# A hybrid decoder trunk: the Strassen products of the FFN's second matrix in another order and with other signs, the sums of its blocks formed by accumulating DMA loads

## The chip, the cores and the metric

One core of one Trainium2 chip. The metric is device time in microseconds (us) of one execution of the whole program; lower is better. The kernel before takes 2162.08 us (median of 3 runs, 2161.11 to 2162.54).

## The reference

Two layers (an mLSTM mixer in the first, a Mamba-2 mixer in the second), each between two half-step SwiGLU FFNs, so four FFNs in all; batch 1, 512 tokens, model width 1024, FFN width 2816, all float32. The change touches the FFN alone:

```python
def swiglu(h, w1, w3, w2):
    return (jax.nn.silu(h @ w1) * (h @ w3)) @ w2

def sublayer(x, fn, g_pre, g_post, shift, scale, gate, weight):
    hmod = rms_norm(x, g_pre) * (1 + scale[:, None, :]) + shift[:, None, :]
    y = rms_norm(fn(hmod), g_post)
    return x + weight * gate[:, None, :] * y
```

## The kernel before

Every matmul is three float32r matmuls (`mm3`, L184 to L188): each operand is split into a high part (ScalarE's copy, L191 or L174) and a low part (VectorE's subtraction, L192 or L175), and high by high, low by high and high by low are added in PSUM. Weights come through a pool of 4 buffers (`rawp`, 128 x 1024 floats, 512 KB) by loads on the SP queue, are split into `wh` and `wl` (pools of 3) or into held slots, and the `raw` buffer is free once VectorE's subtraction has read it. The Tile scheduler orders each engine's instructions; the engines then run them in that order and wait on semaphores.

An FFN (class `Ffn`) has two stages.

**The up-projections** (`first`, `rest`, `tile_in`): 22 tiles of 128 of the FFN's width, each 48 matmuls for w1 and w3. A pair of tiles j (11 pairs) makes an operand of 512 tokens by 256 for w2. `factors(j)` forms the token-side factors of a Strassen scheme over two token halves by two tiles and splits them; three are used at once, four are kept.

**The products with w2.** w2's rows of a pair j fall into two tiles e, its columns into two halves c, so there are four blocks of 128 x 512 floats (256 KB), written here B[e,c]. DRAM holds them as `w2[l, h, c, j]`, a row of 1024 floats for both tiles e. Each of the seven Strassen products is 6 matmuls of 128 x 512 for each j (two token blocks by `mm3`). PSUM has eight banks: four `aux` and four `mm`.

- `flush` (L670 to L687), once for each j while the up-projections run: loads w2(0,j) and w2(1,j) (two loads of 512 KB), adds B00 to B01 (L679), adds B11 to B00 and to B10 (L681, one instruction over 1024), splits, and makes products 1, 7 and 6.
- `outp`, after the last tile (here called the tail): `five(j)` loads B11 (256 KB) for product 5; the loop with L732 loads w2(1,j), subtracts B11 from B01 and makes product 3; the loop with L753 and L759 loads w2(0,j), subtracts B00 from B10 and makes product 4, and for four of the j at once product 2 (of B00). For the other seven j (`HELD = 7`) B00's split is held in slots, and their product 2 comes last, for one token block after the other.
- Between them VectorE and ScalarE combine the PSUM banks into the output rows (L722 to L724, L738 to L740, L767 to L783). `Post.evac` and `Post.finish` square, sum, scale and add to x; `Pre.tok` then transposes the new x on TensorE (L346) for the next stage, whose first weights' matmuls run on the first half of the tokens (`HA`) before the second (`HB`).

So the tail's TensorE work is 4 products for 11 pairs and one last `flush` of 3: 47 x 6 = 282 matmuls. GpSimd (POOL) makes no DMA.

```python
        def halves(self, raw, n=2 * T):
            wh = whp.tile([P, 1024], F32R, tag="wh", name="wh")
            wl = wlp.tile([P, 1024], F32R, tag="wl", name="wl")
            split(wh[:, :n], wl[:, :n], raw[:, :n])
            return [(wh[:, k * T:k * T + T], wl[:, k * T:k * T + T]) for k in range(n // T)]
```

Of the kernel before, what the change touches and what calls it, by code (L numbers as in the profile page):

```python
# [9 lines left out]
F32 = mybir.dt.float32  # L10
# [5 lines left out]
P = 128  # L16
# [19 lines left out]
HELD = 7  # L36
# [20 lines left out]
def trunk(ctx: ExitStack, tc: tile.TileContext, i: dict, out: bass.AP):  # L57
# [475 lines left out]
    class Ffn:  # L533
# [91 lines left out]
        def factors(self, j):  # L625
# [5 lines left out]
            tt(raw[:, :T], s0, s1, ALU.add)  # L631
            tt(raw[:, T:T + H], s0[:, lo], s1[:, hi], ALU.add)
# [5 lines left out]
            for n, (m, src) in enumerate(((1, raw[:, T:T + H]), (6, s0[:, hi]), (7, s1[:, lo]))):  # L638
# [4 lines left out]
            for (ma, a), (mb, b) in (((5, raw[:, lo]), (3, s0[:, lo])), ((2, raw[:, hi]), (4, s1[:, hi]))):  # L643
# [14 lines left out]
        def w2(self, c, j):  # L658
            raw = rawp.tile([P, 1024], F32, tag="raw", name="raw")
            nc.sync.dma_start(raw, i["w2"][self.l, self.h, c, j])  # L660
            return raw

# [40 lines left out]

        def outp(self, nxt):
            n = NF // 2
            m5 = [ps_mm(0), ps_mm(1)]

            def five(j):
                raw = rawp.tile([P, 1024], F32, tag="raw", name="raw")
                nc.sync.dma_start(raw[:, :T], i["w2"][self.l, self.h, 1, j, :, T:])  # L710
                with tc.high_priority():
                    b5, = self.halves(raw, T)
                self.product(m5, self.kept[j][5], b5, j == 0, j == n - 1)
            for j in range(n - 2):
                five(j)
# [4 lines left out]
            lo, hi = slice(0, T), slice(T, D)  # L720
            for t in range(2):
                act(yg[2 + t][:, hi], m[1][t], AF.Copy)  # L722
                tt(yg[t][:, lo], yg[2 + t][:, hi], m[7][t], ALU.add)
                tt(yg[2 + t][:, hi], yg[2 + t][:, hi], m[6][t], ALU.add)  # L724
            done_ps(*m[1], *m[6])
            for j in range(n - 2, n):
                five(j)
            m3 = [ps_aux(), ps_aux()]
            for j in range(n):
                raw = self.w2(1, j)  # L730
                with tc.high_priority():
                    tt(raw[:, lo], raw[:, lo], raw[:, hi], ALU.subtract)  # L732
                    b3, = self.halves(raw, T)
                self.product(m3, self.kept[j][3], b3, j == 0, j == n - 1)
                free(*self.kept[j]["53"])
            for t in range(2):
                act(yg[t][:, hi], m5[t], AF.Copy)
                tt(yg[t][:, lo], yg[t][:, lo], m5[t], ALU.subtract)  # L738
                tt(yg[t][:, hi], yg[t][:, hi], m3[t], ALU.add)
                tt(yg[2 + t][:, hi], yg[2 + t][:, hi], m3[t], ALU.add)  # L740
                post.evac(t, 1, yg[t][:, hi])
            done_ps(*m3)

            m4, m2 = [ps_aux(), ps_aux()], [ps_mm(2), ps_mm(3)]
            held = {}
            joint = range(3, 3 + 2 * (n - HELD), 2)
            hs = [j for j in range(n) if j not in joint]
            for j in range(n):
                raw = self.w2(0, j)
                k = self.kept[j]  # L750
                if j in joint:
                    with tc.high_priority():
                        tt(raw[:, hi], raw[:, hi], raw[:, lo], ALU.subtract)  # L753
                        b2, b4 = self.halves(raw)
                    self.product(m4, k[4], b4, j == 0, j == n - 1)
                    self.product(m2, k[2], b2, j == joint[0], False)
                    free(*k["24"])
                    continue
                tt(raw[:, hi], raw[:, hi], raw[:, lo], ALU.subtract)  # L759
                b4 = slot(F32R, "bh"), slot(F32R, "bl")  # L760
                split(*b4, raw[:, hi])
                held[j] = slot(F32R, "bh"), slot(F32R, "bl")
                split(*held[j], raw[:, lo])
                self.product(m4, k[4], b4, j == 0, j == n - 1)
                free(*b4)
# [680 lines left out]
```

## Time and profile before

| what | value |
|---|---|
| time, median of 3 | 2162.08 us |
| time of the profiled execution | 2159.1 us |
| its span | 2157.1 us |
| TensorE (PE) busy | 2061.5 us, 96% |
| VectorE (DVE) busy | 1625.5 us, 75% |
| ScalarE (ACT) busy | 1004.8 us, 47% |
| GpSimd (POOL) busy | 12.5 us, 1% |
| mean DMA rate | 160 GB/s, 346.08 MB |

The profiled execution lies 3 us under the median of the runs. Busy time is a union of an engine's instructions; a matmul of 128 x 512 is recorded with 0.36 to 0.42 us because its end is modelled and it overlaps the next, so the pace is read from counts in a stretch. "Idle before" is an engine's idle time just before instructions of a group, with what ended it. PEclk is the granted clock of TensorE as a share of 2.4 GHz.

### The profile page before, as it was taken

How to read it: one execution, taken by the hardware profiler on the slowest of the kernel's cores; microseconds unless marked ns; L12 is line 12 of the kernel's file. 1: busy time of each engine (PE TensorE's matmuls, PEld its weight loads, DVE VectorE, ACT ScalarE, POOL GpSimd, SP SyncE). 2: the span in 40 equal slices, each digit the busy share in tenths (PEclk: the TensorE clock that was granted, in tenths of full speed). 3: DMA queues.
4: the chain of work that ended last, by engine and by line, in shares of the span. 5: the costliest groups of instructions: out<-in, count | busy, mean ns of one | idle time of the engine just before them, and what ended most of it. 6: DMA issues, size and time to landing. Idle time of an engine off the chain costs nothing.

```text
span 2157.1 us, 28206 instructions
## 1 busy us (share of the span) xinstructions
PE 2061.5 (96%) x10422; PEld 1709.9 (79%) x10422; DVE 1625.5 (75%) x2699; ACT 1004.8 (47%) x1769; POOL 12.5 (1%) x33
## 2 busy tenths in 40 slices
PE   7999998899999999998999999799999999999997
PEld 5888886797789787866987887698788789888875
DVE  8969967857886888769777755878998857555558
ACT  5434434745463333336433433556656655333334
POOL 0000000000000000000000000000000000000000
PEclk9999999999999999998999999999999999999999
DMA  7556756345334677654457534524334332343344
GB/s 275 187 165 234 234 166 234 113 133 163 125 97 148 224 240 228 200 188 154 157 182 251 167 118 161 191 87 136 113 104 128 114 115 79 109 136 121 119 165 157
DMA packets 108986, 346.08 MB, mean 160 GB/s; under 512 B 13545, under 2 KB 13545, under 8 KB 108849
## 3 DMA queue, kind: packets, MB, share of 16 engines
q1 hardware_dynamic: 108848, 344.29, 49.4%
q8 instruction: 81, 1.33, 0.3%
q14 instruction: 57, 0.46, 0.1%
HBM read 342.00 MB, written 2.24 MB: 160 GB/s over the span
## 4 chain that ended last, share of the span: by engine, by line
PE 67%; DVE 15%; DMA 11%; ACT 4%; issue 3%; DVEq 0%; ACTq 0%; SPq 0%
PE mm L186 19%; PE mm L188 19%; PE mm L187 19%; DMA raw<-in_w 8%; DMA raw<-in_ada_w 2%; DVE wl L192 2%; PE aux L186 2%; DVE wl L175 2%; PE aux L187 2%; PE aux L188 2%; DVE acc L208 2%; ACT wh L174 1%; ACT wh L191 1%; PE aux L1156 1%; DVE raw L681 1%
## 5 line engine op out<-in xcount | busy, mean ns | idle before, releaser
L186 PE MATMUL mm<-hm,wh 128*128 128x512 f32 (+1 forms) x2128 | 771.4, 366 | 4.8 <-ACT hm L360 2.6
L188 PE MATMUL mm<-hm,wl 128*128 128x512 f32 (+1 forms) x2128 | 770.4, 363 | 3.3 <-DVE wl L175 3.2
L187 PE MATMUL mm<-hm,wh 128*128 128x512 f32 (+1 forms) x2128 | 770.1, 363 | 0.0
L174 ACT ACTIVATE wh<-raw 128x1024 fp32r<-128x1024 f32 (+1 forms) x294 | 278.8, 957 | 409.1 <-PE mm L187 131.9
L188 PEld LDWEIGHTS mm<-hm,wl 128*128 128x128 f32 x2128 | 404.0, 190 | 67.9 <-DVE wl L175 6.7
L186 PEld LDWEIGHTS mm<-hm,wh 128*128 128x128 f32 x2128 | 403.1, 191 | 69.0 <-ACT hm L360 3.8
L187 PEld LDWEIGHTS mm<-hm,wh 128*128 128x128 f32 x2128 | 404.6, 190 | 60.7 <-issue 1.4
L175 DVE TENSOR_TENSOR wl<-raw,wh 128x1024 fp32r<-128x1024 f32 (+1 forms) x294 | 320.5, 1096 | 118.5 <-ACT wh L174 114.8
L191 ACT ACTIVATE wh<-raw 128x1024 fp32r<-128x1024 f32 (+1 forms) x192 | 145.3, 763 | 299.0 <-PE mm L187 127.8
L192 DVE TENSOR_TENSOR wl<-raw,wh 128x1024 fp32r<-128x1024 f32 (+1 forms) x192 | 162.9, 854 | 48.8 <-ACT wh L191 46.5
L208 DVE SCALAR_TENSOR_TENSOR acc<-raw,csil,acc 128x1024 f32<-128x1024 f32 x112 | 143.5, 1282 | 44.6 <-DMA raw<-in_ada_w 43.9
L598 DVE TENSOR_TENSOR s<-s,mm 128x512 f32<-128x512 f32 (+1 forms) x97 | 59.7, 617 | 129.9 <-PE mm L188 129.9
L679 DVE TENSOR_TENSOR raw<-raw 128x512 f32<-128x512 f32 x44 | 30.4, 691 | 71.7 <-DMA raw<-in_w 71.5
L186 PE MATMUL aux<-wh,th 128*128 128x512 f32 x176 | 70.0, 406 | 10.5 <-ACT wh L191 10.5
L187 PE MATMUL aux<-wl,th 128*128 128x512 f32 x176 | 69.6, 396 | 0.0
L188 PE MATMUL aux<-wh,tl 128*128 128x512 f32 x176 | 69.5, 395 | 0.0
L191 ACT ACTIVATE kh<-s 128x256 fp32r<-128x256 f32 x88 | 36.5, 416 | 57.8 <-DVE s L598 50.5
L597 ACT ACTIVATE s<-mm 128x512 f32<-128x512 f32 (+1 forms) x97 | 51.3, 531 | 23.2 <-PE mm L188 23.2
L186 PE MATMUL mm<-wh,kh 128*128 128x512 f32 x120 | 48.1, 409 | 13.5 <-ACT wh L191 13.5
L187 PE MATMUL aux<-wl,kh 128*128 128x512 f32 x120 | 50.2, 418 | 9.3 <-DVE wl L192 7.8
L681 DVE TENSOR_TENSOR raw<-raw 128x1024 f32<-128x1024 f32 x44 | 53.8, 1222 | 1.1
L1049 DVE SCALAR_TENSOR_TENSOR cv<-mm,c_mb_cw,cv 128x511 f32<-128x511 f32 (+2 forms) x72 | 53.3, 742 | 0.6
(317 smaller groups left out, 3130.3 us busy)
## 6 DMA issues: line engine op xcount, KB each, us to landing
raw<-in_w SPq DMA_DIRECT2D x346, 512.0 KB, 4.3
raw<-in_ada_w SPq DMA_DIRECT2D x128, 512.0 KB, 4.0
raw<-in_mb_wx SPq DMA_DIRECT2D x24, 512.0 KB, 3.6
raw<-in_w SPq DMA_DIRECT2D x44, 256.0 KB, 2.8
a<-in_ada SPq DMA_DIRECT2D x32, 256.0 KB, 5.4
raw<-in_mb_wz SPq DMA_DIRECT2D x16, 512.0 KB, 4.0
bc<-mb_a SPq DMA_DIRECT2D x32, 256.0 KB, 3.4
raw<-in_mb_wout SPq DMA_DIRECT2D x16, 512.0 KB, 3.5
```

Of the source, the lines that this page charges most:

```text
L174: act(hi[:, :b - a], raw[:, a:b], AF.Copy)
L175: tt(lo[:, :b - a], raw[:, a:b], hi[:, :b - a].bitcast(F32), ALU.subtract)
L186: matmul(ps, stat[0], mov[0], start=first, stop=False)
L187: matmul(ps, stat[0], mov[1], start=False, stop=False)
L188: matmul(ps, stat[1], mov[0], start=False, stop=last)
L191: act(dst_h, src, AF.Copy)
L192: tt(dst_l, src, dst_h.bitcast(F32), ALU.subtract)
L208: stt(st["acc"], raw, csil[:, kc:kc + 1], st["acc"], ALU.mult, ALU.add)
L597: act(s[:, a:b], p[0][:, a:b], AF.Silu)
L598: tt(s[:, a:b], s[:, a:b], p[1][:, a:b], ALU.mult)
L681: tt(two, two, r1[:, T:].unsqueeze(1).to_broadcast([P, 2, T]), ALU.add)
L1049: stt(t[:, s:], ps[:, :T - s], w(k), t[:, s:], ALU.mult, ALU.add)
```

## The change

The scheme's signs are changed so that three of the sums of w2's blocks have plus signs only: product 3 takes B01 + B11, product 4 B10 + B00, product 6 B01 + B00. Product 2 keeps B00. Products 5, 1 and 7 are now the ones made in `flush`, with B11, B00 - B11 and B10 + B11. Product 6 moves from `flush` to the tail, product 5 from the tail to `flush`.

A plus-only sum is made by the loads: `blocks` loads one block of two pairs j at once (256 rows of 2 KB) on the SP queue, and then a second DMA, issued by GpSimd, adds the other block to it in SBUF (`accum_op=ALU.add`). It waits until the first load has landed; ScalarE and VectorE wait until the second has. In the tail VectorE adds no blocks any more.

`outp` now runs product 3 in groups of two pairs, product 4 in groups with product 6's weights loaded and held in between, the first two token blocks' end, product 6, product 2 for the first three groups, and product 2 for the last three groups (`HELD = 3`, now counted in groups) held and last.

```diff
-HELD = 7
+HELD = 3
...
         def flush(self):
...
-                    self.m = {1: [ps_aux(), ps_aux()], 6: [ps_aux(), ps_aux()], 7: [ps_mm(2), ps_mm(3)]}
-                settle()
-                r0, r1 = self.w2(0, j), self.w2(1, j)
+                    self.m = {1: [ps_aux(), ps_aux()], 5: [ps_aux(), ps_aux()], 7: [ps_mm(2), ps_mm(3)]}
+                r0, r1 = self.blocks((0, None), [j]), self.blocks((1, 1), [j])
                 with tc.high_priority():
-                    tt(r1[:, :T], r1[:, :T], r0[:, :T], ALU.add)
-                    two = r0.rearrange("p (a b) -> p a b", b=T)
-                    tt(two, two, r1[:, T:].unsqueeze(1).to_broadcast([P, 2, T]), ALU.add)
+                    b5, = self.halves(r1, T)
+                    tt(r0[:, :T], r0[:, :T], r1[:, :T], ALU.subtract)
+                    tt(r0[:, T:], r0[:, T:], r1[:, :T], ALU.add)
                     b1, b7 = self.halves(r0)
-                    b6, = self.halves(r1, T)
...
-                for m, b in ((1, b1), (7, b7), (6, b6)):
+                for m, b in ((5, b5), (1, b1), (7, b7)):
                     self.product(self.m[m], a[m], b, n == 0, n == NF // 2 - 1)
+                settle()
...
+        def blocks(self, k, js, plus=None):
+
+            raw = rawp.tile([P, 1024], F32, tag="raw", name="raw")
+            if k[1] is None:
+                nc.sync.dma_start(raw, i["w2"][self.l, self.h, k[0], js[0]])
+                return raw
+            part = lambda c, e: i["w2"][self.l, self.h, c, js[0]:js[-1] + 1, :, e * T:e * T + T].rearrange("j p t -> p j t")
+            dst = raw[:, :len(js) * T].rearrange("p (j t) -> p j t", t=T)
+            nc.sync.dma_start(dst, part(*k))
+            if plus is not None:
+                nc.gpsimd.dma_start(dst, part(*plus), accum_op=ALU.add)
+            return raw
+
+        def sums(self, ps, m, k, plus, js):
+
+            raw = self.blocks(k, js, plus)
+            with tc.high_priority():
+                bs = self.halves(raw, len(js) * T)
+            for j, b in zip(js, bs):
+                self.product(ps, self.kept[j][m], b, j == 0, j == NF // 2 - 1)
+
+        def hold(self, k, js, plus=None):
+            raw, held = self.blocks(k, js, plus), []
+            for e in range(len(js)):
+                held.append((slot(F32R, "bh"), slot(F32R, "bl")))
+                split(*held[e], raw[:, e * T:e * T + T])
+            return held
+
         def outp(self, nxt):
...
+            m3 = [ps_mm(0), ps_mm(1)]
+            for js in groups[:3]:
+                self.sums(m3, 3, (1, 0), (1, 1), js)
             while self.pairs or self.pending:
                 self.step()
...
+            for js in groups[3:]:
+                self.sums(m3, 3, (1, 0), (1, 1), js)
...
-                    tt(raw[:, lo], raw[:, lo], raw[:, hi], ALU.subtract)
-                    b3, = self.halves(raw, T)
...
-                tt(raw[:, hi], raw[:, hi], raw[:, lo], ALU.subtract)
-                b4 = slot(F32R, "bh"), slot(F32R, "bl")
-                split(*b4, raw[:, hi])
...
+            m4, held = [ps_aux(), ps_aux()], []
+            for js in groups:
+                self.sums(m4, 4, (0, 1), (0, 0), js)
+                for j in js:
+                    free(*self.kept[j]["34"])
+                held += self.hold((1, 0), js, (0, 0))
...
+            m6 = [ps_mm(2), ps_mm(3)]
+            for j in range(n):
+                self.product(m6, self.kept[j][6], held[j], j == 0, j == n - 1)
+                free(*held[j])
...
+            for js in groups[:-HELD]:
+                self.sums(m2, 2, (0, 0), None, js)
+                for j in js:
+                    free(*self.kept[j]["62"])
+            for js in groups[-HELD:]:
+                held.update(zip(js, self.hold((0, 0), js)))
```

How it moves instructions, at the three places that matter here. First, GpSimd's queue between the start (its constants) and the first mixer (its masks), that is through the first FFN's tail. Before:

```order
L1293 TENSOR_SCALAR c_mb_cb<-c_mb_cb 128x24
L1295 TENSOR_SCALAR c_mb_A<-c_mb_A 32x1
L1293 TENSOR_SCALAR c_mb_nw<-c_mb_nw 128x16
L867 MEMSET lacc 32x512
L909 AFFINE_SELECT st<-st 128x128 x16
```

In the change:

```order
L1300 TENSOR_SCALAR c_mb_nw<-c_mb_nw 128x16
L710 DMA raw<-in_w 128x2x512 x5
L710 DMA raw<-in_w 128x512
L710 DMA raw<-in_w 128x2x512 x10
L710 DMA raw<-in_w 128x512 x2
L874 MEMSET lacc 32x512
L916 AFFINE_SELECT st<-st 128x128 x16
```

18 accumulating DMAs are new there (3 products of 6 groups, the sixth group a single pair), and 18 in each of the other three tails.

Second, VectorE in the first FFN's tail, where product 3 ran (before) and where products 4 and 6 run (change). The number behind a name is its instance. Before:

```order
L732 TENSOR_TENSOR raw_3131<-raw_3131 128x512
L192 TENSOR_TENSOR wl_3122<-raw_3118,wh_3121 128x512
L738 TENSOR_TENSOR yg_3068<-yg_3068,mm_2926 128x512
L732 TENSOR_TENSOR raw_3144<-raw_3144 128x512
L192 TENSOR_TENSOR wl_3135<-raw_3131,wh_3134 128x512
L732 TENSOR_TENSOR raw_3157<-raw_3157 128x512
L192 TENSOR_TENSOR wl_3148<-raw_3144,wh_3147 128x512
```

In the change:

```order
L192 TENSOR_TENSOR wl_3157<-raw_3153,wh_3156 128x1024
L192 TENSOR_TENSOR bl_3176<-raw_3172,bh_3175 128x512
L192 TENSOR_TENSOR bl_3180<-raw_3172,bh_3179 128x512
L192 TENSOR_TENSOR wl_3187<-raw_3183,wh_3186 128x1024
L192 TENSOR_TENSOR bl_3206<-raw_3202,bh_3205 128x512
L192 TENSOR_TENSOR bl_3210<-raw_3202,bh_3209 128x512
```

The block adds (L732) are gone and the splits stand back to back, one of product 4 (`wl`), two held ones of product 6 (`bl`).

Third, TensorE at the end of the first FFN's tail, at the transposes of the new x (`aux<-ident,yg`). Before:

```order
L186 MATMUL mm<-bh,kh 128x512
L187 MATMUL mm<-bl,kh 128x512
L188 MATMUL mm<-bh,kl 128x512
L346 MATMUL aux<-ident,yg 128x128 x16
L186 MATMUL mm<-hm,wh 128x256 x3
```

In the change:

```order
L186 MATMUL mm<-wh,kh 128x512
L187 MATMUL mm<-wl,kh 128x512
L346 MATMUL aux<-ident,yg 128x128 x8
L188 MATMUL mm<-wh,kl 128x512
L186 MATMUL mm<-wh,kh 128x512
```

and, 16 matmuls further on:

```order
L186 MATMUL mm<-wh,kh 128x512
L187 MATMUL mm<-wl,kh 128x512
L188 MATMUL mm<-wh,kl 128x512
L346 MATMUL aux<-ident,yg 128x128 x8
L186 MATMUL mm<-hm,wh 128x256 x2
```

The 16 transposes of the first two token blocks stood behind the last of 42 held matmuls of product 2. Now 8 of them stand behind 35 matmuls of product 6 and 20 of product 2, the other 8 behind 16 more, and the 30 held matmuls of product 2 (`mm<-bh,kh`) have moved in among the next stage's first matmuls (`mm<-hm,wh`), with 69 of these behind the last of them and ahead of the next transposes.

## Rows read from the trace of the kernel before

**Rows 1.** The page, part 1: busy us, share of the span, instructions.
```profile
PE 2061.5 (96%) x10422; PEld 1709.9 (79%) x10422; DVE 1625.5 (75%) x2699; ACT 1004.8 (47%) x1769; POOL 12.5 (1%) x33
```
**Rows 2.** Windows, the four FFNs' up-projections (`rest`): stretch, length, busy us (instructions), PEclk, DMA share, GB/s.
```profile
127.00:310.00 183.00, 182.06 (x842) 149.30 (x842) 149.45 (x214) 71.40 (x118) 0.00 (x0) 1.00 0.64 209
690.00:925.00 235.00, 229.91 (x1090) 187.94 (x1089) 182.65 (x247) 87.90 (x138) 0.00 (x0) 1.00 0.65 213
1080.00:1307.00 227.00, 225.44 (x1031) 184.67 (x1030) 155.06 (x219) 83.17 (x132) 0.00 (x0) 1.00 0.53 173
1850.00:2079.00 229.00, 229.00 (x1011) 189.41 (x1010) 126.00 (x195) 83.90 (x137) 0.00 (x0) 1.00 0.40 123
```
**Rows 3.** Windows, the four tails: PE, PEld, DVE, ACT, POOL, then PEclk, DMA share, GB/s.
```profile
310.00:406.00 96.00, 79.68 (x324) 60.99 (x323) 77.03 (x135) 49.50 (x92) 0.00 (x0) 0.93 0.56 186
925.00:1020.00 95.00, 79.69 (x320) 61.13 (x319) 77.28 (x137) 49.59 (x93) 0.00 (x0) 0.91 0.58 189
1307.00:1405.00 98.00, 81.27 (x332) 61.95 (x331) 78.07 (x139) 51.89 (x97) 0.00 (x0) 0.92 0.55 183
2079.00:2157.00 78.00, 58.67 (x236) 43.59 (x234) 62.06 (x105) 32.87 (x60) 0.00 (x0) 0.93 0.54 182
```
**Rows 4.** Windows, the second tail's middle (products 3, 4 and 2).
```profile
960.00:999.00 39.00, 34.06 (x131) 25.79 (x132) 34.50 (x50) 19.84 (x30) 0.00 (x0) 0.91 0.79 265
```
**Rows 5.** Groups of instructions: TensorE's idle time before the tail's products (busy, mean ns, idle before, releasers).
```profile
L186 PE MATMUL aux<-wh,th 128*128 128x512 f32 x176 | 70.0, 406 | 10.5 <-ACT wh L191 10.5
L187 PE MATMUL aux<-wl,kh 128*128 128x512 f32 x120 | 50.2, 418 | 9.3 <-DVE wl L192 7.8
L187 PE MATMUL mm<-wl,kh 128*128 128x512 f32 x120 | 49.3, 411 | 0.8 <-DVE wl L192 0.7
L186 PE MATMUL mm<-wh,kh 128*128 128x512 f32 x120 | 48.1, 409 | 13.5 <-ACT wh L191 13.5
L186 PE MATMUL aux<-wh,kh 128*128 128x512 f32 x120 | 42.5, 397 | 1.4 <-ACT wh L191 1.3
```
**Rows 6.** The same view: the transposes, and the next stage's first matmuls.
```profile
L346 PE MATMUL aux<-ident,yg 128*128 128x128 f32 x160 | 24.6, 299 | 19.7 <-DVE yg L341 19.5
L186 PE MATMUL mm<-hm,wh 128*128 128x256 f32 x576 | 162.1, 291 | 3.1 <-ACT hm L360 2.6 <-ACT s L597 0.6
```
**Rows 7.** The same view, shapes apart: adds of blocks and splits.
```profile
L192 DVE TENSOR_TENSOR wl<-raw,wh 128x1024 fp32r<-128x1024 f32 x60 | 73.3, 1222 | 6.4 <-ACT wh L191 5.0
L191 ACT ACTIVATE wh<-raw 128x1024 fp32r<-128x1024 f32 x60 | 63.7, 1061 | 158.7 <-DVE raw L681 75.0 <-PE mm L187 56.8 <-DVE raw L753 16.0
L681 DVE TENSOR_TENSOR raw<-raw 128x1024 f32<-128x1024 f32 x44 | 53.8, 1222 | 1.1
L679 DVE TENSOR_TENSOR raw<-raw 128x512 f32<-128x512 f32 x44 | 30.4, 691 | 71.7 <-DMA raw<-in_w 71.5
L732 DVE TENSOR_TENSOR raw<-raw 128x512 f32<-128x512 f32 x44 | 30.3, 688 | 10.4 <-DMA raw<-in_w 10.2
```
**Rows 8.** The page, part 6: DMA issues, KB each, median us to landing.
```profile
raw<-in_w SPq DMA_DIRECT2D x346, 512.0 KB, 4.3
raw<-in_w SPq DMA_DIRECT2D x44, 256.0 KB, 2.8
```
**Rows 9.** The chain that ended last, first tail's end: start us, us, what.
```profile
385.74 0.61 DVE yg L767
...
395.89 0.66 DVE yg L341
```

More of the change, by code (lines that the diff above doesn't have):

```diff
@@ L630, in factors @@
             raw = ygp.tile([P, D], F32, tag="yg", name="traw")
-            tt(raw[:, :T], s0, s1, ALU.add)
-            tt(raw[:, T:T + H], s0[:, lo], s1[:, hi], ALU.add)
+            tt(raw[:, :T], s0, s1, ALU.subtract)
+            tt(raw[:, T:T + H], s0[:, lo], s1[:, hi], ALU.subtract)
             tt(s0[:, hi], s0[:, hi], s0[:, lo], ALU.subtract)
@@ L637, in factors @@
             early = {}
-            for n, (m, src) in enumerate(((1, raw[:, T:T + H]), (6, s0[:, hi]), (7, s1[:, lo]))):
+            for n, (m, src) in enumerate(((1, raw[:, T:T + H]), (7, s1[:, lo]), (5, raw[:, lo]))):
                 c = slice(n * H, n * H + H)
@@ L702, in rest @@
                     pump(int((f - start + 1) * rate) - int((f - start) * rate), False)
+        def blocks(self, k, js, plus=None):
[21 more added lines that the diff above has]
+            return held
         def outp(self, nxt):
             n = NF // 2
[L706 to L715, printed above, removed]
+            groups = [range(j, min(j + 2, n)) for j in range(0, n, 2)]
+            lo, hi = slice(0, T), slice(T, D)
+            m3 = [ps_mm(0), ps_mm(1)]
+            for js in groups[:3]:
+                self.sums(m3, 3, (1, 0), (1, 1), js)
             while self.pairs or self.pending:
@@ L719, in outp @@
             m, yg = self.m, post.yg
-            lo, hi = slice(0, T), slice(T, D)
             for t in range(2):
                 act(yg[2 + t][:, hi], m[1][t], AF.Copy)
+                act(yg[t][:, hi], m[5][t], AF.Copy)
                 tt(yg[t][:, lo], yg[2 + t][:, hi], m[7][t], ALU.add)
[L724 to L728, printed above, removed]
@@ L729, in outp @@
-            for j in range(n):
-                raw = self.w2(1, j)
-                with tc.high_priority():
-                    tt(raw[:, lo], raw[:, lo], raw[:, hi], ALU.subtract)
-                    b3, = self.halves(raw, T)
-                self.product(m3, self.kept[j][3], b3, j == 0, j == n - 1)
-                free(*self.kept[j]["53"])
+                tt(yg[t][:, lo], yg[t][:, lo], yg[t][:, hi], ALU.add)
+            done_ps(*m[1], *m[5])
+            for js in groups[3:]:
+                self.sums(m3, 3, (1, 0), (1, 1), js)
@@ L746, in outp @@
[L746 to L752, printed above, removed]
-                        tt(raw[:, hi], raw[:, hi], raw[:, lo], ALU.subtract)
[L754 to L759, printed above, removed]
-                b4 = slot(F32R, "bh"), slot(F32R, "bl")
-                split(*b4, raw[:, hi])
[L762 to L765, printed above, removed]
+            m4, held = [ps_aux(), ps_aux()], []
@@ L772, in outp @@
                 post.finish(t)
+            m6 = [ps_mm(2), ps_mm(3)]
+            for j in range(n):
+                self.product(m6, self.kept[j][6], held[j], j == 0, j == n - 1)
+                free(*held[j])
+            for t in range(2):
+                tt(yg[2 + t][:, hi], yg[2 + t][:, hi], m6[t], ALU.add)
+            m2, held = [ps_mm(0), ps_mm(1)], {}
+            for js in groups[:-HELD]:
[4 more added lines that the diff above has]
+                held.update(zip(js, self.hold((0, 0), js)))
             for t in range(2):
                 c = slice(t * P, (t + 1) * P)
-                for j in hs:
+                for j in held:
                     ah, al = self.kept[j][2]
-                    mm3(m2[t], (ah[:, c], al[:, c]), held[j], False, j == hs[-1])
+                    mm3(m2[t], (ah[:, c], al[:, c]), held[j], False, j == n - 1)
                     if t:
-                        free(*self.kept[j]["24"], *held[j])
+                        free(*self.kept[j]["62"], *held[j])
                 u = 2 + t
```

13 lines of the change are left out of this document (2 added, 11 removed).

## The prediction

> **What bounds the kernel now.** I read the page's first part, then TensorE's idle time by group, then windows over the four FFNs, then the DMA issues. TensorE is busy 96% of the span [rows 1], so only its own work or its waits can move the time. In the four up-projection stretches it is busy from end to end at full clock; in the last of them 229.00 us over 1011 matmuls is 0.2265 us for one [rows 2], the pace used below. DVE is busy there too (149 of 183 us in the first), but nothing waits for it long. What the change takes from `flush` on DVE in these stretches, 0.53 us for each pair (0.691 + 1.222 for its adds before, two adds of 0.69 now [rows 7]), is therefore hidden, and I count it at nothing; if it were not, 40 flushes would give 21 us.
>
> The tails are another matter. Over their four windows TensorE is idle 16.3, 15.3, 16.7 and 19.3 us, and its granted clock is only 0.91 to 0.93 [rows 3]. At two levels, 2.4 and 1.2 GHz, that is 57 us at the lower one, 28.6 us of lost clock. In the middle of a tail DVE is busy 34.50 of 39 us [rows 4]: there a product needs an add and a subtraction from DVE, 0.69 us each, for 6 x 0.2265 = 1.36 us of matmuls. DVE is as slow as TensorE and stands ahead of it in a chain.
>
> **The change, part by part.** TensorE's work is the same: seven products of 6 matmuls for each pair, 282 of them in a tail, 63.9 us. What changes is what it waits for.
>
> *Waits on DVE's adds, gained.* The groups that start a product in the tails are idle for 10.5, 9.3, 0.8, 13.5 and 1.4 us [rows 5], 35.5 us together: the last flush waiting for two adds and a split, product 3 for its low part, products 4 and 2 for their first split. With the adds gone from the tail, DVE does 4 splits a pair where it did 4 splits and 2 adds; the last flush starts with product 5, which needs no add. I take all 35.5 us, and put the waits that remain into the cost of the loads.
>
> *The seam to the next stage, partly gained.* The transposes are idle 19.7 us and the next stage's first matmuls 2.6 us behind `hm` [rows 6], in three tails. From product 4's combination to DVE's scaling of the first block takes 395.89 + 0.66 - 385.74 = 10.8 us [rows 9]; before, 42 matmuls (9.5 us) stood in between, now 55 (12.5 us), then 16 more ahead of the second block. That covers it: 19.5 us of the 22.3 us go. But the last two blocks' chain, as long as this one, has now only 69 half-width matmuls ahead of its transposes, 69 x 0.113 = 7.8 us: late by 3 us, three times. Net 10.5 us gained.
>
> *Clock.* With fewer stalls part of the 28.6 us comes back. What of it overlaps the idle time just counted no row tells. I take 12 us, and 0 and 28.6 us as its ends.
>
> So the gains are 35.5 + 10.5 + 12 = 58 us, if every sum of blocks were there when wanted.
>
> *The loads, the cost.* A tail loads 7 blocks a pair where it loaded 5, and 18 of its 24 buffers now need two DMAs in a row, the second from GpSimd, which makes no DMA in the kernel before: no row shows its price. Bounds, for one buffer of two pairs. First by the engines' time: 265 GB/s at a share of 0.79 [rows 4] is 335 GB/s with all engines busy, so 0.524 MB takes 1.56 us. If adding costs what loading costs, a buffer takes 3.13 us; if the adding DMA holds the engines twice as long, since it has to read both addends, 4.7 us. Second by the life of a buffer, of which there are four: landing 4.3 us [rows 8], landing of the adding DMA 4.3 us at least, ACT's split 1.06 and DVE's 1.22 us [rows 7] make 10.9 us, a quarter is 2.7 us; with an adding DMA of 8.6 us it is 3.8 us. So one buffer every 3.1 to 4.7 us. I take 3.6: with an adding DMA half as dear again as a load, the engines give 1.56 x 2.5 = 3.9 us and the life (4.3 + 6.5 + 2.3) / 4 = 3.3 us, and of the two the life rests on measured landings.
>
> TensorE uses a buffer up in 12 x 0.2265 = 2.72 us, so it waits only where loads have no lead. In product 3 (5.5 full buffers, with a flush of 4.1 us and the last tile's 10.9 us ahead of most of them) there is lead enough: 5.5 x 3.6 + 2 for the flush's own blocks = 22 us against 15 + 4 + 8. In products 4 and 6 there is not: 11 full buffers, 39.6 us, against 132 matmuls, 29.9 us, and about 4 us of lead from the buffers loaded while product 3 ends. That is 5.7 us of waiting, and 1.5 us for the split that heads each stretch: 7.2 us a tail, 29 us in all. Product 2's plain loads (1.56 us a buffer) keep ahead. ACT does the same number of splits as before and is busy half of a tail [rows 3]; SP issues 46 loads for each FFN instead of 55, GpSimd has nothing else to do in the tails.
>
> **Sum.** 58 gained, 29 paid: 29 us less. The profiled execution takes 2159.1 us, so 2130; the median of the runs lies 3.0 us above it, so I predict **2133 us**.
>
> The rule by which I place the zero: a tail gains 14.5 us, so it is even at 11p - 33.9 + 1.5 = 14.5, a buffer every p = 4.26 us.
>
> **Rivals.**
> *The loads hide.* At 3.13 us a buffer products 4 and 6 wait 0.5 us, with the heads 2 us a tail, 8 us in all: 50 us less, 2112; with all of the clock back 2096. For it: packets have room, the DMA share is 0.54 to 0.58 in the tails [rows 3]. Against it: the life of a buffer uses a median landing measured at that half load.
> *Adding reads twice.* The adding DMA holds the DMA engines for both reads, 4.7 us a buffer. Its place is the pairs of products 4 and 6: 51.7 - 33.9 = 17.8 us of waiting, 1 us in product 3, 1.5 at the heads, 20.3 us a tail, 81 in all: 23 us slower, 2185. It decides from 4.26 us a buffer, an adding DMA of 2.7 us of engine time. For it: the engines run at a share of 0.79 in one such stretch already [rows 4], with fewer bytes. Against it: a DMA engine may have its second read, which is from SBUF, under the first. The Trainium skill ("Collectives: The Full Stack", "The bandwidth ceiling: the fold count and why AG ≠ RS ≠ AR") says that the DMA's add costs nothing itself but needs two source reads on one ring, so that a summing transfer runs at about half the rate of a copy; by that rule this rival holds, but no row here shows an adding DMA.
> *One adding DMA at a time.* If GpSimd's DMAs do not overlap one another, each buffer costs a landing and its issue, 4.3 + 1 us (the 1 us is a guess): 58.3 - 33.9 = 24.4 us in products 4 and 6, 4 us in product 3, 1.5: 30 us a tail, 120 in all, 62 slower, 2224. For it: nothing; it is one engine that issues them. Against it: loads on SP overlap, four to the pool.
> *No change.* The loads cost what the adds cost, p near 4.26 us: within 4 us of 2162.
>
> **How the numbers follow.** My forecast's band (p from 3.2 to 4.2, 2115 to 2159) has 0.45, the hidden loads 0.13, no change 0.08, reading twice 0.22, one at a time 0.12. Faster by over 0.2% (4.3 us, about what a measurement of this kernel can tell from no change) is 0.45 + 0.13 = 0.58, within it 0.08, slower 0.34. The range runs from the hidden loads with most of the clock back, 2100, to 2210, half-way between reading twice without the 12 us of clock (2197) and one at a time; outside lie one at a time and the cheapest end, less than 2 in 10. The faster cases alone, which hold more than half, span 2100 to 2159.
>
> **What would show it.** Right: GpSimd's 72 DMAs land 5 to 8 us after issue; DVE is 84 us less busy (44 x 1.91: for each pair adds of 0.691, 1.222 and twice 0.69 become two of 0.69); TensorE's idle time before `aux<-wh,th` and the transposes shrinks to a few us; its idle in the tails stands before the first matmuls of products 4 and 6, ended by ACT or DVE splits that themselves waited for a DMA; the tails' DMA share rises above 0.75. Wrong: if ACT waits for adding DMAs through all of product 4 and 6 and the clock there falls under 0.9, reading twice or one at a time holds, told apart by whether the DMA share is near 1 or stays low; if the up-projection stretches get shorter, DVE's relief in `flush` was worth what I counted at nothing.

## The result and the profile after

The changed kernel takes **2297.65 us** (median of 4 runs, 2295.77 to 2301.26) against 2161.88 us of the kernel before on the same chip: a ratio of 1.063, 95% interval 1.0612 to 1.0649. It is 136 us slower. The forecast was 2133 us, range 2100 to 2210: wrong in direction and outside the range.

The page of the profiled execution after, parts 1 and 3 (engine busy time; then each DMA queue with its packets, MB and share of the time of 16 engines):

```profile
span 2294.3 us, 28125 instructions
...
PE 2097.7 (91%) x10422; PEld 1735.1 (76%) x10422; DVE 1545.0 (67%) x2575; ACT 1006.3 (44%) x1741; POOL 96.3 (4%) x105
...
q0 software_dynamic: 18048, 34.61, 9.4%
```

Against [rows 1] TensorE does the same 10422 matmuls but is busy 36 us longer (its granted clock over the span is 0.960, before 0.984) and idle 101 us longer (196.6 us where it was 95.6). DVE has lost 80.5 us, as the change says, and now waits more itself. GpSimd issues the adding DMAs; q0 is their queue.

Where the idle time stands, by groups of TensorE's instructions (count, busy, mean ns, idle before, releasers); it answers to [rows 5, 6]:

```profile
L186 PE MATMUL aux<-wh,th 128*128 128x512 f32 x176 | 68.3, 391 | 0.0
...
L186 PE MATMUL mm<-wh,kh 128*128 128x512 f32 x136 | 57.0, 420 | 9.7 <-ACT wh L191 9.2 <-DVE s L598 0.5
...
L186 PE MATMUL aux<-wh,kh 128*128 128x512 f32 x88 | 46.2, 560 | 118.9 <-ACT wh L191 118.9
...
L346 PE MATMUL aux<-ident,yg 128*128 128x128 f32 x160 | 23.2, 292 | 17.2 <-DVE yg L341 17.0
```

One group holds nearly all that is new: the first matmuls of product 4 (`aux<-wh,kh`), 118.9 us. In the kernel before the group of this name, product 3's and four of product 4's, had 1.4, and the other seven of product 4 (`aux<-bh,kh`) had none. Product 3 (`mm<-wh,kh`, with product 2) waits little, and the last flush (`aux<-wh,th`) not at all, where it waited 10.5. ACT is named, but ACT is not the cause. Its own waits say what it stood for:

```profile
ACT wh L191 <- DMA raw<-in_w: 201.9, 40, 11.5
...
ACT bh L191 <- DMA raw<-in_w: 89.6, 20, 6.9
```

Columns: total us, times, longest. The loads were late, so the next view is GpSimd's time line in the middle of the first tail (start, length, idle before and what ended it):

```profile
347.42 1.22 POOL L710 DMA_DIRECT2D raw<-in_w  x1 [6.82 <-issue]
353.80 1.21 POOL L710 DMA_DIRECT2D raw<-in_w  x1 [5.16 <-issue]
360.53 1.22 POOL L710 DMA_DIRECT2D raw<-in_w  x1 [5.52 <-issue]
367.78 1.21 POOL L710 DMA_DIRECT2D raw<-in_w  x1 [6.03 <-issue]
374.25 1.22 POOL L710 DMA_DIRECT2D raw<-in_w  x1 [5.25 <-issue]
380.63 1.21 POOL L710 DMA_DIRECT2D raw<-in_w  x1 [5.17 <-issue]
...
393.39 2.15 POOL L710 DMA_DIRECT2D raw<-in_w  x2 [5.15 <-issue]
```
```profile
raw<-in_w POOLq DMA_DIRECT2D x60, 512.0 KB, 6.1
```

The full adding DMAs (256 rows) of products 4 and 6 start 6.4 to 7.3 us apart in these rows, 6.3 us a buffer over the four tails, and each lands a median 6.1 us after its issue (the last line, from the page's part 6): never two full ones under way. The last row holds two issues back to back: a full one and the half one (128 rows) of the single pair go out together. "issue" as releaser means that the profile shows nothing that GpSimd waited for, neither a buffer nor a load. The DMA view of the same stretch, 355 to 395 us (the mean busy share of 16 engines in 40 slices, then by queue):

```profile
DMA  1899999869992029999307999803999600899900
...
q0 software_dynamic: 1632, 3.15, 50.7%
q1 hardware_dynamic: 1648, 3.15, 20.9%
```

Two things are to be seen. The engines fall idle between one adding DMA and the next (the zeros). And the same 3.15 MB take 50.7% of the engines' time when added and 20.9% when loaded: 6.4 against 2.7 us of all 16 engines for a MB. Windows over the middles of the four tails (as [rows 3], TensorE's busy time first, then at the end PEclk, DMA share and GB/s):

```profile
355.00:395.00 40.00, 21.72 (x64) 16.19 (x64) 10.37 (x14) 8.11 (x14) 7.71 (x8) 0.71 0.72 158
...
2220.00:2260.00 40.00, 21.49 (x66) 15.95 (x65) 8.41 (x11) 7.25 (x10) 7.90 (x7) 0.74 0.75 162
```

TensorE works barely half the time, at a granted clock of 0.71 to 0.76, while no DMA queue, DVE or ACT is full. That is the picture of a chain, not of a full resource.

### The profile page after: what moved, and what is told of

The parts are those of the page before. It is cut to its first block, busy times and chain, and to the rows that moved or that the text cites. A ratio compares the mean times of both kernels' runs of the same rounds, so it can differ in the third digit from the quotient of the medians.

```text
span 2294.3 us, 28125 instructions
## 1 busy us (share of the span) xinstructions
PE 2097.7 (91%) x10422; PEld 1735.1 (76%) x10422; DVE 1545.0 (67%) x2575; ACT 1006.3 (44%) x1741; POOL 96.3 (4%) x105
## 3 DMA queue, kind: packets, MB, share of 16 engines
q0 software_dynamic: 18048, 34.61, 9.4%
## 4 chain that ended last, share of the span: by engine, by line
PE 62%; DMA 14%; DVE 10%; issue 9%; ACT 4%; POOL 1%; SPq 0%; DVEq 0%; POOLq 0%; ACTq 0%
PE mm L186 18%; PE mm L188 18%; PE mm L187 18%; DMA raw<-in_w 10%; DMA raw<-in_ada_w 3%; DVE wl L175 2%; DVE wl L192 2%; PE aux L186 1%; PE aux L187 1%; PE aux L188 1%; ACT wh L191 1%; ACT wh L174 1%; DVE acc L208 1%; POOL raw L710 1%; PE aux L1163 1%
## 5 line engine op out<-in xcount | busy, mean ns | idle before, releaser
L174 ACT ACTIVATE wh<-raw 128x1024 fp32r<-128x1024 f32 (+1 forms) x294 | 278.0, 957 | 383.7 <-PE mm L187 148.7
L175 DVE TENSOR_TENSOR wl<-raw,wh 128x1024 fp32r<-128x1024 f32 (+1 forms) x294 | 320.2, 1098 | 112.2 <-ACT wh L174 110.2
L191 ACT ACTIVATE wh<-raw 128x1024 fp32r<-128x1024 f32 (+1 forms) x148 | 134.3, 907 | 382.3 <-DMA raw<-in_w 201.9
L192 DVE TENSOR_TENSOR wl<-raw,wh 128x1024 fp32r<-128x1024 f32 (+1 forms) x148 | 153.1, 1034 | 198.7 <-ACT wh L191 198.5
L710 POOL DMA_DIRECT2D raw<-in_w x72 | 84.2, 1223 | 1873.0 <-DVE kl L192 1159.1
L186 PE MATMUL aux<-wh,kh 128*128 128x512 f32 x88 | 46.2, 560 | 118.9 <-ACT wh L191 118.9
L186 PEld LDWEIGHTS aux<-wh,kh 128*128 128x128 f32 x88 | 21.3, 262 | 132.2 <-ACT wh L191 128.7
L192 DVE TENSOR_TENSOR bl<-raw,bh 128x512 fp32r<-128x512 f32 x64 | 42.3, 688 | 88.7 <-ACT bh L191 87.0
L191 ACT ACTIVATE bh<-raw 128x512 fp32r<-128x512 f32 x64 | 37.3, 623 | 107.1 <-DMA raw<-in_w 89.6
L191 ACT ACTIVATE kh<-s 128x256 fp32r<-128x256 f32 x132 | 54.5, 413 | 60.0 <-DVE s L598 53.3
```

What stands on the lines that cost most here:

```text
L174: act(hi[:, :b - a], raw[:, a:b], AF.Copy)
L175: tt(lo[:, :b - a], raw[:, a:b], hi[:, :b - a].bitcast(F32), ALU.subtract)
L186: matmul(ps, stat[0], mov[0], start=first, stop=False)
L191: act(dst_h, src, AF.Copy)
L192: tt(dst_l, src, dst_h.bitcast(F32), ALU.subtract)
L710: nc.gpsimd.dma_start(dst, part(*plus), accum_op=ALU.add)
```

## Experiments

Four theories could be told apart: (a) adding DMAs go one after another, because GpSimd has room for the descriptors of one only; (b) an added byte costs the DMA engines twice or more; (c) two landings for each buffer, with four buffers, are too long whatever the second DMA does; (d) the new order itself is worse.

### Take the second DMA away: is the new order worth anything?

```
-            if plus is not None:
-                nc.gpsimd.dma_start(dst, part(*plus), accum_op=ALU.add)
```

The sums of products 3, 4 and 6 are left out; every other instruction stays. It also moves 35 MB less than the change, so it gives the most that the new order could be worth.

> The second DMA is left out altogether, so the sums of blocks in products 3, 4 and 6 are left out. It measures what the new order would gain if every sum were there when wanted. The prediction's terms: 58 us less than before, 2104 us, TensorE idle before the tails' products near 0 where it was 35.5 us, the seam's wait about 12 us where it was 22.3. If the gain is much smaller, the prediction's gains were wrong too, not only its cost of the loads.

Measured: 2094.77 us (one run; the kernel before beside it 2165.13, 2156.34 to 2168.59, 7 runs), 70 us less. So (d) falls: the order and the signs, with the loads for nothing, are worth 64.6 us of span. Its page, part 1, and two groups of TensorE's instructions:

```profile
span 2092.5 us, 27943 instructions
...
PE 2037.7 (97%) x10422; PEld 1702.2 (81%) x10422; DVE 1545.0 (74%) x2575; ACT 1010.0 (48%) x1743; POOL 11.8 (1%) x33
```
```profile
L186 PE MATMUL aux<-wh,kh 128*128 128x512 f32 x88 | 34.1, 400 | 6.5 <-ACT wh L191 6.4
...
L346 PE MATMUL aux<-ident,yg 128*128 128x128 f32 x160 | 21.5, 277 | 7.4 <-DVE yg L341 7.2
```

Idle time is 54.8 us where it was 95.6 [rows 1], 40.8 us less, and TensorE's busy time is 23.8 us less: the clock, 0.996 over the span against 0.984.

### Let the second DMA overwrite instead of add

```
-                nc.gpsimd.dma_start(dst, part(*plus), accum_op=ALU.add)
+                nc.gpsimd.dma_start(dst, part(*plus))
```

Same DMAs, same bytes, same order on GpSimd; the sums are left out. One thing more changes: its packets are 4096 bytes long where the adding DMA's are 2048, so there are half as many, and the room for descriptors (below) may be less of a limit too.

> The second DMA of a sum stays on GpSimd, but overwrites instead of adding, so the sums of blocks in products 3, 4 and 6 are left out. It takes the adding away and leaves GpSimd's issue, its wait and the second transfer. Theory A (room in the ring): if a plain DMA needs as much room as an adding one, still one at a time, about 4.5 to 5 us apart (6.4 less 16 x 94 ns), some 2220 us; if it needs less, they overlap, under 3.2 us apart, 2100 to 2130 us. Rival B (the adding is what is slow): packets of 84 ns instead of 178, under 3.2 us apart, 2100 to 2130 us. Rival C (GpSimd's own path is slow, whatever the ring and the adding): still 6 us apart, about 2290 us.

Measured: 2174.23 us (one run), 79 us above the run without second DMAs and 9 above the median of the kernel before beside it (2165.13). It fits none of the three theories of the expectation. So a second DMA for each buffer already takes back what the new order gains, and probably a little more, without any adding. That is (c), but its two parts, the second landing and the second DMA's bytes, are not taken apart by any run. The DMA queues' part of its page:

```profile
q0 software_dynamic: 9600, 34.61, 4.6%
```

The same 34.61 MB take 4.6% of the engines' 2172.5 us here and 9.4% of 2294.3 us when added: 2.2 times as much. This is (b); with packets of the same 2048 bytes, the adding and the loading queue above gave 2.4 times. The size agrees with the rule weighed in the prediction (the Trainium skill, "Collectives: The Full Stack", "The bandwidth ceiling: the fold count and why AG ≠ RS ≠ AR"), by which a summing transfer needs two reads and runs at about half the rate of a copy. The page says it of a reduce-scatter between cores; that two reads are the reason here too, no run shows.

### More room for descriptors, or smaller adding DMAs

Twice the room that the program sets aside for GpSimd's DMA descriptors:

```
-    nc = bacc.Bacc(..., dynamic_dma_scratch_size=1024)
+    nc = bacc.Bacc(..., dynamic_dma_scratch_size=2048)
```

> The changed kernel with GpSimd's descriptor ring doubled (dynamic_dma_scratch_size 1024 to 2048), nothing else. In the changed kernel GpSimd's adding DMAs start 6.3 to 6.5 us apart in products 4 and 6, each when the one before has ended, and the trace shows nothing that GpSimd waits for. Theory A: the ring has no room for a second one; with twice the ring two are under way, the distance falls to the DMA engines' own time, 16 packets x (84 + 178) ns = 4.2 us a buffer, and the time to about 2160 us. Rival B: the DMA engines or the adding itself allow no more, whatever the ring: 2298 us, 6.4 us apart. Rival C: the four weight buffers bound it: 2298 us, with loads that start late.

Measured: 2230.6 us (2218.25 to 2232.98), ratio to before 1.0297, interval 1.0255 to 1.034: 67 us of the change's 136 us come back. GpSimd's rows at the start, in the middle and at the end of the first tail's products 4 and 6, and the landing:

```profile
331.95 1.20 POOL L710 DMA_DIRECT2D raw<-in_w  x1 [4.03 <-issue]
...
357.87 3.90 POOL L710 DMA_DIRECT2D raw<-in_w  x3 [7.89 <-DMA raw<-in_w]
...
375.26 3.02 POOL L710 DMA_DIRECT2D raw<-in_w  x3 [8.90 <-DMA raw<-in_w]
```
```profile
raw<-in_w POOLq DMA_DIRECT2D x60, 512.0 KB, 8.0
```

Three full DMAs now go out back to back in 3.9 us, at a landing time of 8.0: they overlap. Over the four tails a buffer takes 4.2 to 4.6 us, about the 4.2 that theory A expected, but the time is 70 us above its 2160. Why is said in the last part of the account of the prediction. And, with the room as it was, each adding DMA cut in two:

```
-                nc.gpsimd.dma_start(dst, part(*plus), accum_op=ALU.add)
+                for e in range(len(js)):
+                    nc.gpsimd.dma_start(raw[:, e * T:e * T + T], i["w2"][self.l, self.h, plus[0], js[e], :, plus[1] * T:plus[1] * T + T], accum_op=ALU.add)
```

> The changed kernel with each adding DMA cut in two, one for each pair j, so that each has half the rows; the computation is the changed kernel's. Theory (an adding DMA waits on GpSimd until there is room for its descriptors, and the room holds one of 256 rows): two half DMAs are under way at once, GpSimd's issues come some 3 us apart where they came 6.4 us apart, and the time falls towards that of the run with twice the room: 2220 to 2260 us. Rival (GpSimd, or the DMA engines, do one adding DMA after another whatever its size): each half pays its own start and landing, 2300 us or more.

Measured: 2227.89 us (one run). Two unlike edits, more room for whole DMAs and half the rows in the same room, give the same time, which a limit of one DMA at a time on GpSimd or on its queue would not allow. GpSimd's time line with half DMAs:

```profile
366.64 0.86 POOL L711 DMA_DIRECT2D raw<-in_w  x1 [2.77 <-issue]
368.46 0.88 POOL L711 DMA_DIRECT2D raw<-in_w  x1 [0.95 <-issue]
369.72 0.88 POOL L711 DMA_DIRECT2D raw<-in_w  x1 [0.38 <-issue]
371.04 0.86 POOL L711 DMA_DIRECT2D raw<-in_w  x1 [0.45 <-issue]
```

Issues come 1.3 to 1.8 us apart where they came 6.4 apart, at a landing time of 6.3 us. So (a) holds: with room 1024 two DMAs of 256 rows did not fit together. Both edits together:

> The half adding DMAs with twice the room for descriptors as well. Halving alone (2228 us) and twice the room alone (2231 us) gave the same. If room were still what holds the adding DMAs back, both together go on falling, to 2190 to 2210 us. If what is left is the adding packets' time on the DMA engines and the four buffers, each held for two landings, it stays within 10 us of them: 2218 to 2240 us.

Measured: 2235.04 us (one run), no further gain. What is left there is not room. Windows over 350 to 385 us, first of the run with twice the room, then of the run that overwrites, then of the run without second DMAs, where this stretch already holds products 6 and 2 and the next stage:

```profile
350.00:385.00 35.00, 23.01 (x77) 17.00 (x77) 12.15 (x16) 9.72 (x17) 7.86 (x7) 0.79 0.94 211
```
```profile
350.00:385.00 35.00, 28.09 (x104) 22.11 (x103) 15.52 (x23) 15.78 (x25) 4.74 (x7) 0.85 0.74 254
```
```profile
350.00:385.00 35.00, 34.71 (x175) 28.80 (x174) 30.24 (x59) 25.77 (x46) 0.00 (x0) 1.00 0.53 176
```

With the room given, the DMA engines are at a share of 0.94 and move only 211 GB/s: full, with bytes that cost twice. When the second DMA overwrites they are at 0.74 and move 254, and GpSimd's row below shows it waiting for first loads to land, which themselves need a free buffer: there the life of the four buffers is the likely limit (a fifth was not tried, so this is argued, not shown).

```profile
328.83 0.71 POOL L710 DMA_DIRECT2D raw<-in_w  x1 [3.22 <-issue]
...
350.78 0.73 POOL L710 DMA_DIRECT2D raw<-in_w  x1 [8.17 <-DMA raw<-in_w]
...
366.94 0.55 POOL L710 DMA_DIRECT2D raw<-in_w  x1 [0.24 <-issue]
```

The first and the last of these rows begin and end the first tail's second DMAs of products 4 and 6: 38.1 us for ten and a half buffers, 3.6 us a buffer (3.6 to 3.8 in the four tails). Together this is a stair: 2094.8 us without second DMAs, 79 more for the second DMA as such, 56 more for adding, 67 more for one at a time. Its first two steps rest on one run each.

### The same sums on DVE

Two plain loads and an add on DVE in place of load and adding DMA:

```
-                nc.gpsimd.dma_start(dst, part(*plus), accum_op=ALU.add)
+                more = rawp.tile([P, 1024], F32, tag="raw", name="more")
+                nc.sync.dma_start(more[...], part(*plus))
+                tt(raw[:, :n], raw[:, :n], more[:, :n], ALU.add)
```

> The new order and signs, but the sums are formed by two plain loads on SP into two buffers and an add on VectorE (1.22 us for two pairs), no DMA on GpSimd. A tail then loads 42 buffers of 512 KB, 1.56 us each by the prediction's rate, 65 us against 64 us of matmuls, and VectorE has 18 adds more, 22 us, beside 27 us of splits. If the prediction's gains hold and the loads about keep up: 2115 to 2150 us, faster than before. If four buffers, now two for a sum, are too few: (4.3 + 1.22 + 1.06 + 1.22) / 2 = 3.9 us a sum, products 4 and 6 wait 10 us a tail, about 2150 us.

Measured: 2194.63 us (2190.32 to 2195.04), ratio 1.0139, interval 1.0117 to 1.0162. Better than the runs with adding DMAs so far, outside both expectations, still slower than before: it loads as many blocks as the change and takes two buffers for each sum. So the next edit makes the tail load 6 blocks a pair: for products 4 and 6 one 512 KB transfer brings B00 and B10 of a pair, another B01 of two pairs, so that B00 is loaded once for both sums; product 3 loads both its blocks in one transfer, and DVE adds in place:

```
+        def both(self, ps, js):
+            r1, held = self.blocks((1, 0), js), []
+            for e, j in enumerate(js):
+                r0, c = self.blocks((0, None), [j]), slice(e * T, e * T + T)
+                nc.vector.tensor_tensor(r1[:, c], r1[:, c], r0[:, :T], op=ALU.add)
...
+                    nc.vector.tensor_tensor(r0[:, T:], r0[:, T:], r0[:, :T], op=ALU.add)
...
```

> The changed kernel's order and signs without adding DMAs and with 5 blocks loaded for each pair instead of 7: product 3 loads both its blocks in one 512 KB transfer and DVE adds its halves; for products 4 and 6 one 512 KB transfer brings both blocks of a pair, a second one the third block of two pairs, and DVE makes both sums. If the cost of the run with plain loads and DVE adds (2194.6 us) lay in its loads (two 512 KB buffers for each sum of two pairs, four buffers in all), this one comes back to 2130 to 2160 us, since three buffers serve two pairs of products 4 and 6 where four did. If it lay in DVE (4 splits and 4 adds for two pairs, about 5.2 us against 5.4 us of matmuls), it stays at 2180 us or more.

(The expectation leaves out product 2's block: it is 6 for a pair instead of 7.) Measured: 2163.98 us (2158.14 to 2168.72, 10 runs), ratio 1.0011, interval 0.9994 to 1.0028: equal to the kernel before. DVE is as busy as in the run ahead (1630.4 against 1624.6 us), so the loads and their buffers were most of that run's cost. What is left looks like DVE: in 350 to 385 us it is busy 30.43 of 35 us. DVE's time line at the seam:

```profile
373.94 1.28 DVE L778 TENSOR_TENSOR yg<-yg,aux 128x512 f32<-128x512 f32 x2 [0.47 <-PE aux L188]
375.15 1.22 DVE L192 TENSOR_TENSOR wl<-raw,wh 128x1024 fp32r<-128x1024 f32 x1
...
387.85 0.74 DVE L341 TENSOR_SCALAR yg<-x,rc 128x1024 f32<-128x1024 f32 x1
```

From product 4's combination to the end of the scaling it takes 14.7 us, against 10.8 in the kernel before [rows 9], with seven splits in between where there were two, and the transposes wait 28.0 us (19.7 before [rows 6]).

Four attempts to relieve DVE there. The sums of product 6 on GpSimd, in that kernel:

```
-                nc.vector.tensor_tensor(r1[:, c], r1[:, c], r0[:, :T], op=ALU.add)
+                nc.gpsimd.tensor_tensor(r1[:, c], r1[:, c], r0[:, :T], op=ALU.add)
```

> As the run before it, but the sums of product 6, which are held for a later stretch, are added on GpSimd. No row shows a GpSimd addition of 128x512. If it takes up to about 2.5 us and leaves DVE alone, DVE is 11 x 0.69 = 7.6 us a tail less busy and the time is 2110 to 2150 us, below the run with all adds on DVE by 10 us or more; if the raw buffers are held longer by it, or DVE's own instructions get longer beside it, no gain or a loss of 10 to 40 us.

Measured: 2201.76 us (2197.94 to 2202.88), ratio 1.0185, interval 1.0165 to 1.0205; a reason is shown with the last edit below. Product 3's sums by adding DMAs, with room 2048, and products 4 and 6 on DVE:

```
-                self.joint(m3, js)
+                self.sums(m3, 3, (1, 0), (1, 1), js)
```

> Products 4 and 6 as in the run with joint loads and DVE adds; product 3's sums by adding DMAs with twice the room for descriptors, so that only 6 adding DMAs are left for each FFN, where three are issued ahead of the last flush. If adding DMAs cost time only where no lead covers them, as the trace of the change shows (118.9 us of idle in product 4, 9.7 in product 3), these cost at most some 10 us over the four tails, and DVE, 7.6 us a tail less busy (11 adds of 0.69 us), is earlier at the seam, where the transposes wait 28 us for it: 2135 to 2155 us, below both kernels. If the second landing slows product 3 as it slows product 4, 2165 to 2200 us.

Measured: 2167.72 us, ratio 1.0043, interval 1.0025 to 1.0062. DVE is 30 us less busy over the kernel and nothing is gained, where 2135 to 2155 us were expected: the transposes still wait 30.5 us. Product 4's combination, scaling and transposes at high priority, in that kernel and in the joint one:

```
+            with tc.high_priority():
...
                     tt(yg[t][:, lo], yg[t][:, lo], m4[t], ALU.add)
...
                     post.evac(t, 0, yg[t][:, lo])
                     post.finish(t)
```

> As the run before it, with product 4's combination, the scaling and the transposes of the first two blocks scheduled with high priority, so that DVE does them ahead of the splits of products 6 and 2. If the 28 us of idle at the transposes are DVE's queue (the scaling stands behind those splits), 10 to 20 us go: 2120 to 2145 us. If TensorE, which runs in order, then stands at transposes that come too early, or its splits are late, no gain or 10 to 20 us lost against that run.

> The run with joint loads and DVE adds (2164.0 us), no adding DMA, with the same high priority for product 4's combination, scaling and transposes. If DVE's queue at the seam is what keeps that run from beating the kernel before, 2140 to 2155 us; if DVE is short of time throughout (28.6 us of splits and adds for 29.9 us of matmuls in products 4 and 6), the wait only moves: 2160 to 2175 us.

Measured: 2169.9 us (ratio 1.0044, interval 1.0028 to 1.0061) and 2166.32 us (1.0024, 1.0012 to 1.0037): the waits at the transposes stay at 29.6 and 28.9 us. But the edit moved nothing. In both runs every engine's instructions stand in the same order as without it, and DVE's rows at the seam of the second (compare those above) show it:

```profile
375.47 1.28 DVE L779 TENSOR_TENSOR yg<-yg,aux 128x512 f32<-128x512 f32 x2 [0.48 <-PE aux L188]
376.75 1.23 DVE L192 TENSOR_TENSOR wl<-raw,wh 128x1024 fp32r<-128x1024 f32 x1
...
389.80 0.74 DVE L341 TENSOR_SCALAR yg<-x,rc 128x1024 f32<-128x1024 f32 x1
```

So these two only repeat the runs ahead of them, within 2.4 us. Whether the scaling's place in DVE's queue holds the seam was not tested; what holds it stays open, and that it is not product 3's adds alone is all that the runs say. Last, the kernel before with its tail's subtractions on GpSimd:

```
-                    tt(raw[:, lo], raw[:, lo], raw[:, hi], ALU.subtract)
+                    nc.gpsimd.tensor_tensor(raw[:, lo], raw[:, lo], raw[:, hi], op=ALU.subtract)
...
```

> The kernel before with the subtractions of product 3 and of products 4 and 2 in the tail (22 a tail, 0.69 us each on DVE) moved to GpSimd, nothing else. If GpSimd takes up to about 1.4 us for one and leaves DVE alone, the waits of products 3, 4 and 2 on DVE shrink: 24 us of idle at most, 2140 to 2155 us. If it takes about 2 us or more, the chain load, add, split gets longer than the four buffers cover: 2170 to 2220 us.

Measured: 2180.39 us, ratio 1.0089, interval 1.0064 to 1.0115. GpSimd's cost for one, in this run (by groups, product 3's subtraction) and in the run with product 6's sums:

```profile
L732 POOL TENSOR_TENSOR raw<-raw 128x512 f32<-128x512 f32 x44 | 64.6, 1476 | 1712.1 <-DMA raw<-in_w 1706.0 <-DVE wl L192 5.8 <-DVE yg L738 0.3
```
```profile
L733 POOL TENSOR_TENSOR raw<-raw 128x512 f32<-128x512 f32 x44 | 68.5, 1562 | 1804.3 <-DMA raw<-in_w 1368.8 <-DVE wl L192 422.6 <-DVE yg L459 12.9
```

At 1.48 to 1.56 us, where DVE takes 0.69 [rows 7], GpSimd keeps a buffer 0.8 us longer for each add. And it does not leave DVE alone, as both expectations asked. DVE's splits of held blocks, in the kernel before and with its subtractions on GpSimd:

```profile
L192 DVE TENSOR_TENSOR bl<-raw,bh 128x512 fp32r<-128x512 f32 x56 | 36.6, 683 | 0.0
```
```profile
L192 DVE TENSOR_TENSOR bl<-raw,bh 128x512 fp32r<-128x512 f32 x56 | 62.1, 1131 | 4.2 <-ACT bh L191 3.5
```

By the single instructions of that trace, the 25 splits beside which GpSimd computed nothing took 0.68 us, the 31 others 1.49. So 88 subtractions of 0.69 us, 61 us, left DVE, and its busy time fell by 8 us, from 1625.5 to 1617.4. In the run with product 6's sums on GpSimd it fell by 9 us where 30 were moved. How much of the loss is the slower splits and how much the longer life of a buffer, no run tells apart. No version here beats the kernel before with all of the sums made.

## Why the prediction was wrong, step by step

**What bounds the kernel: right.** Waits and clock in the tails were the only thing to win or lose. The up-projection stretches kept their pace: 803 matmuls in 127 to 300 us without second DMAs, 801 in the change, 798 before. DVE's relief in `flush` was worth nothing, as counted.

**The gains: right in kind, near in size.** Forecast: 46 us of waits and 12 of clock, 58. The run without second DMAs gains 40.8 us of idle time and 23.8 of busy time, 64.6. Of the five groups of [rows 5] 7.8 us are left, of the transposes' 19.7 us [rows 6] 7.4. The clock term, for which I took 12 between 0 and 28.6, came out near the upper end. So the nearness of the sum is partly luck: the waits gave 5 us less than forecast, the clock 12 more.

**The loads, the cost: the step that failed.** It took 3.6 us for one buffer and 29 us in all; the second DMAs cost 202 us (2294.3 less 2092.5 of span). Three things were wrong in it.

First, the size: a buffer of products 4 and 6 takes 6.3 us, outside the bounds of 3.1 to 4.7. Those bounds rested on the DMA engines' time and on the buffers' life. What ended last was a third thing, the room for GpSimd's descriptors, and no row of the trace before could show it, since GpSimd issued no DMA there. I had it as the rival "one adding DMA at a time", at 2224 us and a chance of 0.12, and wrote that nothing spoke for it. Its landing of 4.3 us plus a guess of 1 us was too small: 6.1 us measured, and a gap. With 6.3 us in its own formula, that rival comes to some 2267 us, still 31 short of the result.

Second, I took an adding DMA as half as dear as a load again, a value between two ends with no row nearer to either; it is 2.2 to 2.4 times as dear, the price of the rival "adding reads twice" (that it is the reading is not shown). Both rivals' costs are there, one on top of the other: with the room mended the engines are full at 0.94. The sign named to tell them apart decided it rightly for the change itself: share 0.72, so one at a time.

Third, the price of waiting. I set a wait of 1 us at 1 us of time and the clock as a separate gain. In the runs they come together. Against the run without second DMAs, the overwriting run has 51.6 us more idle time and 28.4 us more busy time for the same matmuls; twice the room 84.9 and 49.8; the change 141.8 and 60.0. A microsecond of waiting in these tails costs 1.4 to 1.6 us. By that alone my point of balance was too high: the overwriting run has no adding at all, its buffers in products 4 and 6 come every 3.6 to 3.8 us, about the value I took and well below my 4.26, and at 2174.2 us (one run) it is still some 10 us slower than the kernel before. With twice the room a buffer takes 4.4 us in the mean, inside my bounds; the formula then gives 2169 us, and 2231 were measured. So the loads' cost failed twice over: the time of a buffer lay outside the bounds, and even a buffer inside them cost far more than the formula made of it, most of all in clock (28 and 50 us of TensorE's busy time in these two runs).

**The signs.** Landing 5 to 8 us after issue: 6.1. DVE 84 us less busy: 80.5. `aux<-wh,th` to zero: yes. Idle time before the first matmuls of products 4 and 6: product 4's yes, 118.9 us instead of a few; product 6's (`mm<-bh,kh`) had none. DMA share above 0.75 in the tails: no, 0.70 to 0.75 in their middles, the sign of the slow case. Clock under 0.9 in products 4 and 6, a sign of being wrong: yes, 0.71 to 0.76. The transposes at a few us: no, 17.2, though 7.4 once the second DMAs are gone.

## What to carry to other kernels

An add that rides on a DMA was not free: it took the add from a compute engine, but cost the DMA engines over twice the time of a load and put a second landing into the life of every buffer, so count landings against buffers before bytes against bandwidth. When an engine begins to issue DMAs that it never issued, give "one at a time" real weight, and look first at the distance between its issues: equal distances a little above the landing time, with no releaser named, were the room for descriptors here, and cutting the DMA in two tests that in one run. After an edit that is to reorder instructions, compare the order before reading the time: two runs here changed no instruction's place. And before moving work to an idle engine, look whether the first engine's own instructions get longer beside it. And where a stall lies in dense matmul work, price it with the clock that it costs, here 1.4 to 1.6 times its length in all.

## What the runs showed of the hardware that was not expected

- With the room for descriptors at 1024, only one adding DMA of 256 rows at a time was under way from GpSimd, 6.3 us a buffer; at 2048, or with 128 rows each, they overlapped, and both edits gave 67 to 70 us back. The profile names no wait for it.
- An adding DMA took 2.4 times the engine time of a load of the same bytes in one stretch (50.7% against 20.9% for 3.15 MB each), and 2.2 times that of an overwriting DMA over the kernel. The overwriting DMAs from GpSimd moved their 34.61 MB in 9600 packets, the adding ones in 18048.
- A GpSimd instruction that issues an adding DMA is 1.22 us long, one for half the rows 0.86, and one for an overwriting DMA of the same block 0.72.
- A VectorE split of 128x512 took 0.68 us alone and a mean 1.49 us while GpSimd was subtracting (31 of 56 in that run); VectorE's busy time fell by 8 us where 61 us of subtractions had left it.
